# Splitting the queries before their transposes, keeping the keys in two orders, and one way of splitting the transposed probabilities

## The chip, the cores and the metric

The kernel runs on one core of one Trainium2 chip. The metric is device time in microseconds (us) of one execution; three executions of the kernel before are given, with their median. The engines are called as in the profile: PE (TensorE, matrix products and transposes; PEld is its weight load), DVE (VectorE), ACT (ScalarE), POOL (GpSimd) and SP (which issues the DMAs).

## What is computed

The reference is a two-layer transformer in fp32 on 512 tokens of width 1024, with 16 heads of 64. Layer A mixes tokens with three branches of attention over 4 key groups, layer B with sliding-window attention with sinks over 2 key groups; each is followed by a gated feed-forward network with a short convolution. Cut to the part that the change touches, it is:

```python
# layer A, for each block of 128 queries (selection keeps all 8 blocks of 64 keys here)
sc  = einsum('bgrqd,bgnd->bgrqn', qq, kc_h) * dh ** -0.5       # 31 compressed keys
p_c = softmax(where(valid, sc, NEG)) * valid
ss  = einsum('bgrqd,bgqkcd->bgrqkc', qq, k_sel) * dh ** -0.5   # selected keys, causal
sw  = einsum('bgrqd,bgkd->bgrqk', qq, kwb) * dh ** -0.5        # window of 512 keys
out = g0 * (p_c @ vc_h) + g1 * (softmax(ss) @ v_sel) + g2 * (softmax(sw) @ vwb)
# layer B, for each block of 128 queries and the 256 keys around it
sc  = einsum('bnqgrd,bnkgd->bgrnqk', qb, kk) * dh ** -0.5
p   = exp(sc - mx) / (exp(sc - mx).sum() + exp(sink - mx));  o = p @ vv
```

## The kernel before

Every fp32 product is made of float32r products of a rounded part ("hi") and a rounded remainder ("lo"). `weight` (lines 108 to 118) loads a weight tile with a DMA from SP, has ACT round it to `wh` (line 116) and POOL or DVE subtract to `wl` (line 117); `mm3` (lines 101 to 104) then makes three products.

The core runs, in this order: the first projections of layer A (0 to about 100 us); attention A with the other projections woven in (100 to 350 us); feed-forward A (to 745 us); projections of B and attention B (745 to 890 us); feed-forward B.

A head's 64 numbers fill half of the 128 rows that a product sums over, and the kernel uses the other half for the split. The keys are laid as [hi | lo] along the rows: `cat_k` (line 271) makes the two halves (ACT line 198, POOL line 199), `stack_k` (line 277) transposes them (line 282, float32r) and ACT takes them out of PSUM (line 287). The queries are laid twice, as [q | q]: `dup_q` (line 289) copies and scales them on POOL (line 291), `stack_q` (line 295) transposes the copy in fp32 (line 300), ACT rounds the result out of PSUM to `qh` (line 302) and DVE subtracts to `ql` (line 303). The scores are then two products on the same keys, `qh` and then `ql` (lines 710 and 711 in A, 928 and 929 in B, 672 and 673 for the compressed keys).

A unit of attention is a "quad": four heads on a block of 128 queries. Each layer has 16 of them. Its steps in A are `prepare` (`dup_q`), `stack` (`stack_q`), four `head` steps (scores on PE, max on DVE line 722, exponentials on ACT line 733, scaling on POOL line 740), `weigh` (which ends in the split of `pc`, on ACT line 198 and POOL line 199), and a body: `trans(z)` turns probabilities by four fp32 transposes (`probs_t`, line 310) and splits them into `pth` and `ptl`, `product(z)` multiplies them with the values (lines 761 and 762), `ctrans` turns `pc` (line 769), `finish` writes the heads out. In `probs_t` two ways are built in: "V" rounds out of PSUM on ACT (line 314) and subtracts on DVE (line 315); "P" copies out raw on ACT (`ptr`, line 318) and does both steps on POOL (lines 319 and 320). In A the way "P" is taken where `z % 99 == 1`, once in each quad; in B it is never taken.

`weave` merges lists of steps by places between 0 and 1, and the tables `LEAD_A`, `LAG_A`, `PREP`, `CMP` and `FILL_A` place the heads and `weigh` of the next quad, the `stack` of the one after it and the projections among the body of this one. The program text so written gives priorities; a planner then lays out each engine's queue from them, from its own estimate of each instruction's duration and from the time at which a buffer comes free. Each engine runs its queue in order. Tiles with `bufs=2` alternate between two buffers: a writer waits until the readers of the tile two back are done.

Of the kernel before, what the change touches and what calls it, by code (L numbers as in the profile page):

```python
# [17 lines left out]
P = 128  # L18
S = 512
# [18 lines left out]
SPLIT_A = {'out': 'P', 'rope': 'S', 'ropek': 'S', 'kcat': 'P', 'cmp': 'P', 'stack': 'P', 'every': 99}  # L38
SPLIT_B = {'out': 'P', 'rope': 'S', 'kcat': 'P', 'stack': 'P'}
# [33 lines left out]
def hybrid_kernel(ctx, tc, t):  # L73
# [198 lines left out]
    def cat_k(pool, k, n):  # L272

        kc = pool.tile([P, 2, 2, HD], F32R, name="kcat", bufs=2)
        split_sb(kc[:, :n, 0], kc[:, :n, 1], k, "kcat")
        return kc

    def stack_k(dst, kc, n):

        ps = t_tile()  # L280
        for g in range(n):
            pe_tr(ps[:, g * P:(g + 1) * P].bitcast(F32R), kc[:, g].rearrange("p a d -> p (a d)"), identr)
        src = ps[:, :n * P].rearrange("p (g n) -> p g n", g=n)
        if pick["split"]["stack"] == "V":
            nc.vector.tensor_copy(dst, src)
        else:
            nc.scalar.copy(dst, src)

    def dup_q(pool, q):
        qd = pool.tile([P, 4, 2, HD], F32, name="qd", bufs=2)  # L290
        nc.gpsimd.tensor_scalar(qd, q.unsqueeze(2).to_broadcast([P, 4, 2, HD]), SCALE, 1.0,
                                op0=OP.mult, op1=OP.mult)
        return qd

    def stack_q(pool, qd):
        qh = pool.tile([P, 4, P], F32R, name="qh", bufs=2)
        ql = pool.tile([P, 4, P], F32R, name="ql", bufs=2)
        ps = t_tile()
        for r in range(4):
            pe_tr(ps[:, r * P:(r + 1) * P], qd[:, r].rearrange("p a d -> p (a d)"), ident)  # L300
        pv = ps.rearrange("p (r n) -> p r n", r=4)
        nc.scalar.copy(qh, pv)
        nc.vector.tensor_sub(ql, pv, qh.bitcast(F32))
        return qh, ql

    def probs_t(pool, blocks, way="V"):

# [5 lines left out]
        if way == "V":  # L313
            nc.scalar.copy(ph, ps)  # L314
            nc.vector.tensor_sub(pl, ps, ph.bitcast(F32))  # L315
        else:
            raw = pool.tile([P, S], F32, name="ptr", bufs=2)
            nc.scalar.copy(raw, ps)
            nc.gpsimd.tensor_scalar(ph, raw, 1.0, 1.0, op0=OP.mult, op1=OP.mult)
            nc.gpsimd.tensor_sub(pl, raw, ph.bitcast(F32))  # L320
        return ph, pl
# [128 lines left out]
    with tc.tile_pool(name="att_a", bufs=1) as pa, tc.tile_pool(name="att_a2", bufs=1) as pp:  # L450
        gates = pa.tile([P, NT, NH * 3], F32, name="gates")
        KcT = pa.tile([P, P], F32R, name="KcT")
# [18 lines left out]
        def stack_kg(g):  # L471
            def go(i):
                k0 = 32 + i * 2 * P
                stack_k(K[g][:, k0:k0 + 2 * P].rearrange("p (b n) -> p b n", b=2), kcs[g, i], 2)
# [88 lines left out]
        def compress(kv):  # L563
# [50 lines left out]
            def third():  # L614
                if kv == 0:
                    stack_k(KcT.unsqueeze(1), st["kc"], 1)
# [34 lines left out]
        def quad_a(g, i):  # L651
# [5 lines left out]
            def prepare():  # L657
                st["qd"] = dup_q(pp, Q[g][:, i])

            def stack():  # L660
                st["q"] = stack_q(pp, st["qd"])
# [3 lines left out]
            def compressed():  # L665
                qh, ql = st["q"]
                cs = t_tile()[:, 0:P]
                mm(cs, identb, cmask[:, i].unsqueeze(1).to_broadcast([P, 4, 32]), start=True, stop=False)
                for r in range(4):
                    o = cs[:, r * 32:(r + 1) * 32]  # L670
                    kc = KcT[:, g * 32:(g + 1) * 32]
                    mm(o, qh[:, r], kc, start=False, stop=False)
                    mm(o, ql[:, r], kc, start=False, stop=r == 3)
# [11 lines left out]
            def weigh():  # L685
# [5 lines left out]
                st["pc"] = pp.tile([P, 4, 2, 32], F32R, name="pc", bufs=2)  # L691
                split_sb(st["pc"][:, :, 0], st["pc"][:, :, 1], pcb, "cmp")

            def head(r):
                def go():
                    qh, ql = st["q"]
                    sf = s_tile().rearrange("p a n -> p (a n)")
                    if joint and r == 0:
                        if g not in front:
                            front.add(g)  # L700
                            nc.vector.tensor_copy(K[g][:, 0:32], KcT[:, g * 32:(g + 1) * 32])
# [161 lines left out]
    with tc.tile_pool(name="att_b", bufs=1) as pb:  # L863
# [5 lines left out]
        KB = pb.tile([P, GB, NT, P], F32R, name="KB")  # L869
# [30 lines left out]
        weave([lambda i=i: stack_k(KB[:, :, i], kcs[i], GB) for i in range(NT)],  # L900
              [lambda i=i: evac_qb(0)(i, q0_ps(i)) for i in range(NT)], qproj[1][:2])

        with tc.tile_pool(name="att_b2", bufs=1) as pp:
            ot = [xpool.tile([P, NCH // 2, 2, S], F32R, name=n) for n in ("s0", "s2")]

            def quad_b(q, i):
# [5 lines left out]
                def prepare():  # L912
                    st["qd"] = dup_q(pp, Q[q][:, i])

                def stack():
                    st["q"] = stack_q(pp, st["qd"])

                def scores():
                    qh, ql = st["q"]
                    s2 = s_tile()  # L920
                    kk = KB[:, g, k0:k0 + 2].rearrange("p i n -> p (i n)")
                    mk = band if i > 0 else band0
                    for a in range(2):
                        mm(s2[:, a], identb, mk.unsqueeze(1).to_broadcast([P, 2, 256]), start=True, stop=False)
                        for e in range(2):
                            r = 2 * a + e
                            o = s2[:, a, e * 256:(e + 1) * 256]
                            mm(o, qh[:, r], kk, start=False, stop=False)
                            mm(o, ql[:, r], kk, start=False, stop=e == 1)
# [228 lines left out]
```

## Time and profile before

| what | us |
|---|---|
| median of three executions | 1291.32 (1287.09 to 1292.36) |
| the profiled execution | 1289.82 |
| its span, first to last instruction | 1288.0 |
| PE busy in the span | 1246.4 |
| POOL busy | 671.4 |
| DVE busy | 785.8 |
| ACT busy | 631.2 |

The profile names each group of instructions by line, engine, operation and tile (out<-in). "Busy" adds up the durations, and since products follow each other before the one before has ended, a busy PE need not be a PE at its best rate. The chain of waits goes back from the last instruction and gives each moment to the one thing that everything after it waited for.

### The profile page before, as it was taken

To read this page: it belongs to the slowest core of one execution; us is meant where nothing else is said; L and a number is where in the kernel's file an instruction comes from. 1 tells how busy PE (TensorE), PEld (TensorE's weight loads), DVE (VectorE), ACT (ScalarE), POOL (GpSimd) and SP (SyncE) were. 2 spreads that over 40 slices of the span, in tenths; PEclk is the share of its full clock that TensorE was granted. 3 is DMA by queue.
4 is the path that set the end of the run, shared out by engine and by line. 5 is a ranking of instruction groups with operands and counts; after the bars stand their busy time and mean duration, and the time that the engine had idled before them with its cause. 6 is when DMAs were issued, how large, how long until landed. Compare 5 with 4: busy or idle time off the path is not lost.

```text
span 1288.0 us, 17680 instructions
## 1 busy us (share of the span) xinstructions
PE 1246.4 (97%) x6539; PEld 1034.6 (80%) x6539; DVE 785.8 (61%) x1262; ACT 631.2 (49%) x1280; POOL 671.4 (52%) x604
## 2 busy tenths in 40 slices
PE   8999999989999999999999998999999999999997
PEld 7897887768778888888888897987788888888886
DVE  6866766566448774047776456775487831587712
ACT  5657676777445343124434346775453421344432
POOL 4049696867574444444445446765644444444452
PEclk9999999999999999999999999999999999999999
DMA  5441010210032222222222131121222222222221
GB/s 194 135 160 52 2 50 17 73 60 34 33 100 97 93 88 99 98 94 87 98 98 98 49 116 34 34 78 41 95 98 90 91 98 98 91 89 99 98 82 66
DMA packets 34085, 106.45 MB, mean 83 GB/s; under 512 B 4048, under 2 KB 6608, under 8 KB 34000
## 3 DMA queue, kind: packets, MB, share of 16 engines
q1 hardware_dynamic: 34000, 105.34, 24.3%
q8 instruction: 51, 0.84, 0.3%
q14 instruction: 34, 0.28, 0.1%
HBM read 103.23 MB, written 2.10 MB: 82 GB/s over the span
## 4 chain that ended last, share of the span: by engine, by line
PE 84%; DVE 7%; ACT 3%; POOL 3%; issue 2%; DMA 1%; SPq 0%; DVEq 0%; ACTq 0%; POOLq 0%
PE pss L103 14%; PE pss L104 14%; PE pss L102 14%; PE pst L102 10%; PE pst L104 10%; PE pst L103 10%; PE pst L310 3%; DVE s L185 2%; POOL wl L117 1%; PE psv L762 1%; PE pss L710 1%; PE psv L761 1%; PE pss L711 1%; ACT prm L733 1%; PE pst L300 1%
## 5 line engine op out<-in xcount | busy, mean ns | idle before, releaser
L117 POOL TENSOR_TENSOR wl<-wr,wh 128x1024 fp32r<-128x1024 f32 x164 | 395.7, 2413 | 402.5 <-ACT wh L116 402.5
L116 ACT CAST wh<-wr 128x1024 fp32r<-128x1024 f32 (+2 forms) x201 | 197.6, 984 | 347.0 <-issue 170.7
L103 PE MATMUL pss<-s,wh 128*128 128x512 f32 x736 | 292.0, 397 | 3.8 <-DVE s L185 3.8
L102 PE MATMUL pss<-s,wh 128*128 128x512 f32 x736 | 291.3, 396 | 2.3 <-ACT s L198 2.1
L104 PE MATMUL pss<-s,wl 128*128 128x512 f32 x736 | 290.8, 396 | 0.0
L103 PEld LDWEIGHTS pss<-s,wh 128*128 128x128 f32 x736 | 138.3, 188 | 39.4 <-DVE s L185 6.2
L102 PEld LDWEIGHTS pss<-s,wh 128*128 128x128 f32 x736 | 138.1, 188 | 37.1 <-ACT s L198 3.0
L104 PEld LDWEIGHTS pss<-s,wl 128*128 128x128 f32 x736 | 138.3, 188 | 32.8
L104 PE MATMUL pst<-actv,wl 128*128 128x512 f32 (+1 forms) x363 | 141.0, 389 | 0.0
L103 PE MATMUL pst<-actv,wh 128*128 128x512 f32 (+1 forms) x363 | 140.7, 388 | 0.0
L102 PE MATMUL pst<-actv,wh 128*128 128x512 f32 (+1 forms) x363 | 140.2, 386 | 0.0
L415 DVE SCALAR_TENSOR_TENSOR cv<-u,convp,cv 128x512 f32<-128x512 f32 x88 | 123.3, 1439 | 12.9 <-ACT cv L414 12.9
L199 DVE TENSOR_TENSOR actv<-sa,actv 128x512 fp32r<-128x512 f32 x44 | 101.6, 2312 | 30.7 <-ACT actv L198 30.5
L443 DVE TENSOR_TENSOR s<-s,pst 128x512 f32<-128x512 f32 x31 | 21.3, 687 | 152.6 <-PE pst L104 152.6
L412 DVE TENSOR_TENSOR u<-pss,R 128x512 f32<-128x512 f32 x84 | 54.1, 686 | 65.1 <-PE pss L104 65.1
L420 ACT ACTIVATE sa<-cv 128x512 f32<-128x512 f32 x44 | 27.9, 634 | 123.1 <-DVE cv L417 123.0
L103 PEld LDWEIGHTS pst<-actv,wh 128*128 128x128 f32 x363 | 68.4, 188 | 15.1
L102 PEld LDWEIGHTS pst<-actv,wh 128*128 128x128 f32 x363 | 68.4, 188 | 14.8
L104 PEld LDWEIGHTS pst<-actv,wl 128*128 128x128 f32 x363 | 68.4, 188 | 14.0
L315 DVE TENSOR_TENSOR ptl<-pst,pth 128x512 fp32r<-128x512 f32 x92 | 62.3, 686 | 21.5 <-ACT pth L314 20.7
L314 ACT CAST pth<-pst 128x512 fp32r<-128x512 f32 x92 | 53.8, 592 | 37.1 <-PE pst L310 30.6
L414 ACT ACTIVATE cv<-u,convp 128x512 f32<-128x512 f32 x88 | 66.6, 807 | 2.1 <-DVE u L412 2.1
(242 smaller groups left out, 2583.5 us busy)
## 6 DMA issues: line engine op xcount, KB each, us to landing
wr<-fin SPq DMA_DIRECT2D x88, 512.0 KB, 3.2
wr<-fout SPq DMA_DIRECT2D x44, 512.0 KB, 3.2
wr<-wg SPq DMA_DIRECT2D x10, 512.0 KB, 3.2
wr<-cw SPq DMA_DIRECT2D x8, 512.0 KB, 3.3
wr<-woA SPq DMA_DIRECT2D x8, 512.0 KB, 3.2
wr<-woB SPq DMA_DIRECT2D x8, 512.0 KB, 3.2
wr<-wqb SPq DMA_DIRECT2D x6, 512.0 KB, 3.2
s<-xT SPq DMA_DIRECT2D x8, 256.0 KB, 5.6
```

What stands on the lines that cost most here:

```text
L102: mm(out, ah, bh, start=start, stop=False)
L103: mm(out, ah, bl, start=False, stop=False)
L104: mm(out, al, bh, start=False, stop=stop)
L116: nc.scalar.copy(hi[:, :n], raw[:, :n])
L117: engines[next(pick["w"], "P")].tensor_sub(lo[:, :n], raw[:, :n], hi[:, :n].bitcast(F32))
L199: engines[pick["split"][name] if name else "V"].tensor_sub(lo, src, hi.bitcast(F32))
L310: pe_tr(ps[:, r * P:(r + 1) * P], blocks[r], ident)
L314: nc.scalar.copy(ph, ps)
L315: nc.vector.tensor_sub(pl, ps, ph.bitcast(F32))
L412: nc.vector.tensor_mul(u[:, s, 2:], src, norm["R"])
L414: act(cv[:, s], u[:, s, 2:], AF.Identity, bias=par[:, 3:4], scale=par[:, 2:3])
L415: nc.vector.scalar_tensor_tensor(cv[:, s], u[:, s, 1:S + 1], par[:, 1:2], cv[:, s], op0=OP.mult, op1=OP.add)
```

## The change

The queries are split first: `cat_q` rounds q to hi on ACT and subtracts to lo on POOL, both from and to SBUF, on 128x256 numbers, and lays them as [hi | lo]. `stack_q` transposes that in float32r, and one ACT copy takes it out of PSUM as `qt`. The keys are laid out as [hi | lo | hi] by `cat_k` and transposed at two offsets, so that two orders, [hi | lo] and [lo | hi], stand in `K`, `KB` and `KcT`; one DVE instruction takes both out of PSUM and applies the scale. The scores are two products of the same `qt`, with one order and then the other. All probabilities go the way "V". To make room, `kn` in A and `pc` go from two buffers to one.

```diff
-SPLIT_A = {..., 'kcat': 'P', 'cmp': 'P', 'stack': 'P', 'every': 99}
+SPLIT_A = {..., 'kcat': 'P', 'cmp': 'P'}
     def cat_k(pool, k, n):
-        kc = pool.tile([P, 2, 2, HD], F32R, name="kcat", bufs=2)
-        split_sb(kc[:, :n, 0], kc[:, :n, 1], k, "kcat")
+        kc = pool.tile([P, 2, 3, HD], F32R, name="kcat", bufs=2)
+        nc.scalar.copy(kc[:, :n, 0:3:2], k.unsqueeze(2).to_broadcast([P, n, 2, HD]))
+        engines[pick["split"]["kcat"]].tensor_sub(kc[:, :n, 1], k, kc[:, :n, 0].bitcast(F32))
         return kc
     def stack_k(dst, kc, n):
         ps = t_tile()
-        for g in range(n):
-            pe_tr(ps[:, g * P:(g + 1) * P].bitcast(F32R), kc[:, g].rearrange("p a d -> p (a d)"), identr)
-        src = ps[:, :n * P].rearrange("p (g n) -> p g n", g=n)
-        if pick["split"]["stack"] == "V":
-            nc.vector.tensor_copy(dst, src)
-        else:
-            nc.scalar.copy(dst, src)
-    def dup_q(pool, q):
-        qd = pool.tile([P, 4, 2, HD], F32, name="qd", bufs=2)
-        nc.gpsimd.tensor_scalar(qd, q.unsqueeze(2).to_broadcast([P, 4, 2, HD]), SCALE, 1.0,
-                                op0=OP.mult, op1=OP.mult)
-        return qd
+        for o in range(2):
+            for g in range(n):
+                a = (o * n + g) * P
+                pe_tr(ps[:, a:a + P].bitcast(F32R), kc[:, g].rearrange("p a d -> p (a d)")[:, o * HD:o * HD + P], identr)
+        nc.vector.tensor_scalar(dst, ps[:, :2 * n * P].rearrange("p (o g n) -> p o g n", o=2, g=n), SCALE, None, op0=OP.mult)
+    def cat_q(pool, q):
+        qc = pool.tile([P, 4, 2, HD], F32R, name="qc", bufs=2)
+        nc.scalar.copy(qc[:, :, 0], q)
+        nc.gpsimd.tensor_sub(qc[:, :, 1], q, qc[:, :, 0].bitcast(F32))
+        return qc
-    def stack_q(pool, qd):
-        qh = pool.tile([P, 4, P], F32R, name="qh", bufs=2)
-        ql = pool.tile([P, 4, P], F32R, name="ql", bufs=2)
+    def stack_q(pool, qc):
+        qt = pool.tile([P, 4, P], F32R, name="qt", bufs=2)
         ps = t_tile()
         for r in range(4):
-            pe_tr(ps[:, r * P:(r + 1) * P], qd[:, r].rearrange("p a d -> p (a d)"), ident)
-        pv = ps.rearrange("p (r n) -> p r n", r=4)
-        nc.scalar.copy(qh, pv)
-        nc.vector.tensor_sub(ql, pv, qh.bitcast(F32))
-        return qh, ql
+            pe_tr(ps[:, r * P:(r + 1) * P].bitcast(F32R), qc[:, r].rearrange("p a d -> p (a d)"), identr)
+        nc.scalar.copy(qt, ps.rearrange("p (r n) -> p r n", r=4))
+        return qt
-    def probs_t(pool, blocks, way="V"):
+    def probs_t(pool, blocks):
...
-        KcT = pa.tile([P, P], F32R, name="KcT")
+        KcT = pa.tile([P, 2, P], F32R, name="KcT")
-            K.append(pa.tile([P, 32 + NT * 2 * P], F32R, name="Kg", bufs=2))
+            K.append(pa.tile([P, 2, 32 + NT * 2 * P], F32R, name="Kg", bufs=2))
-                kn = pa.tile([P, 2, HD], F32, name="kn", bufs=2)
+                kn = pa.tile([P, 2, HD], F32, name="kn", bufs=1)
-                st["pc"] = pp.tile([P, 4, 2, 32], F32R, name="pc", bufs=2)
+                st["pc"] = pp.tile([P, 4, 2, 32], F32R, name="pc", bufs=1)
-                        mm(o, qh[:, r], K[g][:, k0 + a:k0 + b], start=True, stop=False)
-                        mm(o, ql[:, r], K[g][:, k0 + a:k0 + b], start=False, stop=b < n0 and not joint)
+                        mm(o, qt[:, r], K[g][:, 0, k0 + a:k0 + b], start=True, stop=False)
+                        mm(o, qt[:, r], K[g][:, 1, k0 + a:k0 + b], start=False, stop=b < n0 and not joint)
-                    pt[z] = probs_t(pp, [st["pr"][r][:, k, b] for r in range(4)],
-                                    "P" if z % SPLIT_A["every"] == 1 else "V")
+                    pt[z] = probs_t(pp, [st["pr"][r][:, k, b] for r in range(4)])
-        KB = pb.tile([P, GB, NT, P], F32R, name="KB")
+        KB = pb.tile([P, 2, GB, NT, P], F32R, name="KB")
```

The compressed scores (lines 672 and 673) and those of B (928 and 929) change as those of A do, the copy of `KcT` to the front of `Kg` (line 701) takes both orders, and `prepare` calls `cat_q` in place of `dup_q`.

## Rows read from the trace of the kernel before

**Rows 1.** The page's first part: busy time of each engine over the span, with its share and the number of instructions.

```profile
PE 1246.4 (97%) x6539; PEld 1034.6 (80%) x6539; DVE 785.8 (61%) x1262; ACT 631.2 (49%) x1280; POOL 671.4 (52%) x604
```

**Rows 2.** Busy time by stretch (us from the span's start, length, then for PE, PEld, DVE, ACT and POOL busy us and instructions, the granted PE clock, DMA share, GB/s): attention A, feed-forward A, attention B in two parts, and then four quarters of attention A.

```profile
100.00:350.00 250.00, 236.75 (x1535) 195.27 (x1534) 154.93 (x384) 172.56 (x514) 186.59 (x277) 0.99 0.12 41
350.00:745.00 395.00, 392.55 (x1735) 318.13 (x1734) 241.18 (x252) 156.28 (x206) 183.52 (x83) 1.00 0.27 91
760.00:780.00 20.00, 17.24 (x135) 15.86 (x133) 13.22 (x39) 9.47 (x31) 13.38 (x14) 1.00 0.23 80
780.00:890.00 110.00, 105.67 (x679) 91.91 (x680) 73.17 (x176) 73.28 (x207) 70.70 (x108) 1.00 0.14 44
...
100.00:125.00 25.00, 22.20 (x145) 17.58 (x144) 16.37 (x51) 20.11 (x68) 23.16 (x39) 0.93 0.19 64
125.00:150.00 25.00, 23.25 (x166) 20.00 (x164) 20.14 (x46) 20.80 (x66) 22.66 (x38) 1.00 0.00 1
175.00:200.00 25.00, 23.84 (x162) 19.17 (x160) 18.09 (x48) 23.11 (x71) 24.19 (x35) 1.00 0.13 43
225.00:250.00 25.00, 22.77 (x175) 19.80 (x174) 14.41 (x45) 17.91 (x56) 23.05 (x34) 1.00 0.13 44
```

**Rows 3.** The chain of waits by line, first in attention A (100 to 350 us), then in attention B (755 to 890 us): share of the stretch.

```profile
by line: PE pst L310 9.7%; PE pst L102 9.5%; PE pst L104 9.0%; PE pst L103 9.0%; PE psv L762 5.7%; PE psv L761 5.7%; PE pss L710 5.7%; PE pss L711 5.0%; ACT prm L733 4.4%; issue 3.8%; POOL wl L117 2.6%; DVE nmx L722 2.4%; POOL prl L740 2.3%
...
by line: PE pst L102 13.4%; PE pst L103 12.7%; PE pst L104 12.6%; POOL wl L117 6.9%; PE pst L310 6.5%; PE pss L929 4.8%; PE pss L928 4.6%; PE psv L963 4.2%; PE psv L962 4.1%; PE pst L300 3.9%; PE pss L924 3.7%; DVE stat L938 3.1%; issue 2.2
```

**Rows 4.** Transposes: first by line, with count and duration in ns (min/median/max); then two neighbouring pieces of the chain of waits at the start of B (start us, us, what), in which each transpose counts from the start of one to the start of the next.

```profile
L300 PEld LDWEIGHTS pst<-cst,qd x128: 137/140/143, 88.1 to 865.2; 128*128 128x128 f32 x128
L300 PE MATMUL pst<-cst,qd x128: 270/272/329, 88.1 to 865.3; 128*128 128x128 f32 x128
L282 PEld LDWEIGHTS pst<-identr,kcat x41: 138/141/237, 74.3 to 766.1; 128*128 128x128 f32 x41
L282 PE MATMUL pst<-identr,kcat x41: 221/228/454, 74.4 to 766.1; 128*128 128x128 f32 x41
...
766.24 0.13 PE pst L282 x2
766.37 0.46 PE pst L300 x4
```

**Rows 5.** Groups by form over the whole span: shapes, count, busy us, mean ns of one, then the idle time before them and what ended it.

```profile
L302 ACT CAST qh<-pst 128x512 fp32r<-128x512 f32 x32 | 19.0, 594 | 9.4 <-PE pst L300 8.8
L303 DVE TENSOR_TENSOR ql<-pst,qh 128x512 fp32r<-128x512 f32 x32 | 21.9, 685 | 5.1 <-ACT qh L302 4.6
L291 POOL TENSOR_SCALAR qd<-Qb 128x512 f32<-128x512 f32 x16 | 10.0, 623 | 9.7 <-PE pst L300 7.6 <-DVE Qb L215 2.0 <-PE pst L310 0.2
L198 ACT CAST s<-osum 128x256 fp32r<-128x256 f32 x32 | 13.2, 412 | 8.6 <-DVE osum L331 8.3
L199 POOL TENSOR_TENSOR s<-osum,s 128x256 fp32r<-128x256 f32 x32 | 23.7, 740 | 19.5 <-ACT s L198 19.5
L319 POOL TENSOR_SCALAR pth<-ptr 128x512 fp32r<-128x512 f32 x16 | 9.9, 620 | 4.3 <-ACT ptr L318 4.0 <-DVE ptl L315 0.2
L320 POOL TENSOR_TENSOR ptl<-ptr,pth 128x512 fp32r<-128x512 f32 x16 | 20.6, 1286 | 0.4
L315 DVE TENSOR_TENSOR ptl<-pst,pth 128x512 fp32r<-128x512 f32 x92 | 62.3, 686 | 21.5 <-ACT pth L314 20.7
L287 ACT CAST Kg<-pst 128x256 fp32r<-128x256 f32 x16 | 6.1, 382 | 0.6 <-PE pst L282 0.6
L198 ACT CAST kcat<-kn 128x128 fp32r<-128x128 f32 x20 | 6.1, 306 | 0.9 <-DVE kn L215 0.5 <-POOL kn L215 0.4
```

**Rows 6.** Pieces of the chain of waits (start us, us, what) in both layers: first the split of the queries on DVE, the first and the last of five pieces (0.60, 0.61, 0.70, 0.70 and 0.61 us); then the copy of the queries on POOL (both pieces); then the two POOL steps of the way "P" (both); then the copy of the keys out of PSUM on ACT (the first and the last of three, 0.27, 0.27 and 0.37 us).

```profile
106.24 0.60 DVE ql L303
803.80 0.61 DVE ql L303
...
98.05 0.59 POOL qd L291
197.06 0.59 POOL qd L291
...
199.15 0.59 POOL pth L319
201.40 1.24 POOL ptl L320
...
181.91 0.27 ACT Kg L287
255.91 0.37 ACT Kg L287
```

**Rows 7.** Instructions in order of time (start us, us, engine, line). The key tile `kn` of the fourth token block and the split of the third and fourth key tiles, at the start of A; then the first and the last of four pairs in which ACT writes the next quad's `pc` before PE has turned this quad's.

```profile
83.15 0.28 DVE L215 TENSOR_TENSOR kn<-rope,rope 128x128 f32<-128x128 f32 x1
87.23 0.91 POOL L199 TENSOR_TENSOR kcat<-kn,kcat 128x128 fp32r<-128x128 f32 x2
...
208.37 0.30 ACT L198 CAST pc<-pcb 128x128 fp32r<-128x128 f32 x1
210.93 0.28 PE L769 MATMUL pst<-identr,pc 128*128 128x128 f32 x2
...
309.97 0.33 ACT L198 CAST pc<-pcb 128x128 fp32r<-128x128 f32 x1
312.27 0.29 PE L769 MATMUL pst<-identr,pc 128*128 128x128 f32 x2
```

More of the change, by code (lines that the diff above doesn't have):

```diff
@@ L37 @@
 W_B = 8 * "V"
-SPLIT_A = {'out': 'P', 'rope': 'S', 'ropek': 'S', 'kcat': 'P', 'cmp': 'P', 'stack': 'P', 'every': 99}
-SPLIT_B = {'out': 'P', 'rope': 'S', 'kcat': 'P', 'stack': 'P'}
+SPLIT_A = {'out': 'P', 'rope': 'S', 'ropek': 'S', 'kcat': 'P', 'cmp': 'P'}
+SPLIT_B = {'out': 'P', 'rope': 'S', 'kcat': 'P'}
 LEAD_A = [0.21, 0.02, 0.72, 0.53, 0.59, 0.42, 0.4, 0.11, 0.02, 0.99, 0.65, 0.43, 0.05, 0.42, 1.02, 0.48]
@@ L312, in probs_t @@
         pl = pool.tile([P, S], F32R, name="ptl", bufs=2)
[L313 to L320, printed above, removed]
+        nc.scalar.copy(ph, ps)
+        nc.vector.tensor_sub(pl, ps, ph.bitcast(F32))
         return ph, pl
@@ L615, in third @@
                 if kv == 0:
-                    stack_k(KcT.unsqueeze(1), st["kc"], 1)
+                    stack_k(KcT.unsqueeze(2), st["kc"], 1)
                     return
@@ L657, in prepare @@
             def prepare():
-                st["qd"] = dup_q(pp, Q[g][:, i])
+                st["qc"] = cat_q(pp, Q[g][:, i])
             def stack():
-                st["q"] = stack_q(pp, st["qd"])
+                st["q"] = stack_q(pp, st["qc"])
                 st["sums"] = small.tile([P, 4, 2], F32, name="sums")
@@ L665, in compressed @@
             def compressed():
-                qh, ql = st["q"]
+                qt = st["q"]
                 cs = t_tile()[:, 0:P]
@@ L670, in compressed @@
                     o = cs[:, r * 32:(r + 1) * 32]
-                    kc = KcT[:, g * 32:(g + 1) * 32]
-                    mm(o, qh[:, r], kc, start=False, stop=False)
-                    mm(o, ql[:, r], kc, start=False, stop=r == 3)
+                    kc = KcT[:, :, g * 32:(g + 1) * 32]
+                    mm(o, qt[:, r], kc[:, 0], start=False, stop=False)
+                    mm(o, qt[:, r], kc[:, 1], start=False, stop=r == 3)
                 csv = cs.rearrange("p (r b) -> p r b", r=4)
@@ L695, in go @@
                 def go():
-                    qh, ql = st["q"]
+                    qt = st["q"]
                     sf = s_tile().rearrange("p a n -> p (a n)")
@@ L700, in go @@
                             front.add(g)
-                            nc.vector.tensor_copy(K[g][:, 0:32], KcT[:, g * 32:(g + 1) * 32])
+                            nc.vector.tensor_copy(K[g][:, :, 0:32], KcT[:, :, g * 32:(g + 1) * 32])
                         st["pcb"] = pp.tile([P, 4, 32], F32, name="pcb", bufs=2)
@@ L899, in hybrid_kernel @@
         warm_exp(r_nat[:, 0:1])
-        weave([lambda i=i: stack_k(KB[:, :, i], kcs[i], GB) for i in range(NT)],
+        weave([lambda i=i: stack_k(KB[:, :, :, i], kcs[i], GB) for i in range(NT)],
               [lambda i=i: evac_qb(0)(i, q0_ps(i)) for i in range(NT)], qproj[1][:2])
@@ L912, in prepare @@
                 def prepare():
-                    st["qd"] = dup_q(pp, Q[q][:, i])
+                    st["qc"] = cat_q(pp, Q[q][:, i])
                 def stack():
-                    st["q"] = stack_q(pp, st["qd"])
+                    st["q"] = stack_q(pp, st["qc"])
                 def scores():
-                    qh, ql = st["q"]
+                    qt = st["q"]
                     s2 = s_tile()
-                    kk = KB[:, g, k0:k0 + 2].rearrange("p i n -> p (i n)")
+                    kk = [KB[:, o, g, k0:k0 + 2].rearrange("p i n -> p (i n)") for o in range(2)]
                     mk = band if i > 0 else band0
@@ L927, in scores @@
                             o = s2[:, a, e * 256:(e + 1) * 256]
-                            mm(o, qh[:, r], kk, start=False, stop=False)
-                            mm(o, ql[:, r], kk, start=False, stop=e == 1)
+                            mm(o, qt[:, r], kk[0], start=False, stop=False)
+                            mm(o, qt[:, r], kk[1], start=False, stop=e == 1)
                     st["sv"] = s2.rearrange("p a (e n) -> p (a e) n", e=2)
```

2 lines of the change are left out of this document (1 added, 1 removed).

## The prediction

> **What bounds the kernel now.** I read the shares of the engines first. PE is busy for 97% of the span [rows 1], so a change must either take work from PE or shorten the few waits that PE has. The next view is busy time by stretch. In feed-forward A PE is idle for 2.5 of 395 us, and nothing of the change lies there. In attention A (100 to 350 us) PE is idle for 13.3 of 250 us, in attention B (760 to 890 us) for 2.8 + 4.3 = 7.1 of 130 us [rows 2]. These two stretches hold all that moves. In four quarters of A POOL is busy for 22.7 to 24.2 of 25 us, and in the same four PE is idle for 2.8 + 1.8 + 1.2 + 2.2 = 8.0 us; in the first of them the granted clock is 0.93, elsewhere in these rows 0.99 or 1.00 [rows 2]. The third view is the chain of waits: in A most of it is PE's own work, and of the shares in the row that are not PE's, ACT has 4.4%, DVE 2.4% and POOL 4.9%; in B POOL's weight splitting has 6.9% and DVE's max 3.1% [rows 3]. So PE's work counts nearly in full, POOL's and DVE's only where they stand on the chain.
>
> **PE's own work.** The scores keep their number, shape and kind of products, so they cost what they did; that both now use one weight tile saves nothing, since `mm3` already uses one tile twice in a row and the trace has as many loads as products [rows 1]. What changes is the transposes. The 128 of the queries go from fp32 to float32r: four fp32 ones take 0.46 us of the chain and two float32r ones 0.13 us [rows 4], so a group of four falls from 0.46 to 0.26, and 32 groups save 6.4 us. The keys get a second set: 16 tiles of A and 4 of B with two more each, and the compressed keys with one more, 41 in all [rows 4], at 0.065 us 2.7 us more. Net 3.7 us less; the piece of 0.46 is a long one, and with the 0.44 that four steps of 0.11 give it is 5.8 - 2.7 = 3.1. PE is busy for 95% of both stretches, so I take **2.9 us less**.
>
> Here a rule speaks against the change. The rows show two float32r transposes in 0.13 us although each has a weight load of 141 ns, as long as the 140 ns of the fp32 kind [rows 4], so the load does not set the pace there. The Trainium skill, page "TensorE: Matmul & The Clock Gate", section "Back-to-back issue gap", says that in a real kernel the spacing of products is set by the load and the product together, and gives about 81 ns at 128 columns. By that figure, an estimate, the queries would save 32 x (0.44 - 0.32) = 3.8 us and the keys cost 3.3, so that almost nothing would be left. The row is of this very instruction and I go by it; the mechanism is a rival below.
>
> **The queries.** On DVE 32 subtractions of 685 ns go, on ACT 32 copies of 256 columns at 412 ns come, on POOL 32 copies of 623 ns become 32 subtractions at 740 ns [rows 5]; the ACT copy out of PSUM stays at 594 ns for `qt` as for `qh`. Scores then wait for one copy in place of a copy and a subtraction. The subtraction stands on the chain five times, 3.2 us together [rows 6], and nothing takes its place: **3.2 us less**, with 0 as the other end if another engine is ready no earlier. The POOL copy is on the chain twice with 0.59 us [rows 6]. There the new steps are 0.41 + 0.74 = 1.15 us, so **1.1 us more**. At the other 30 quads `prepare` runs two quads ahead and that covers it; without that cover it would be 30 x 0.53 = 16 us, but the same cover holds for the present copy. ACT's copy and POOL's subtraction stand in front of the exponentials and of the scaling of the probabilities in their queues.
>
> **The probabilities.** In each of A's 16 quads POOL loses 0.62 + 1.29 us, 30.6 us in all, and DVE gets a subtraction of 686 ns, 11.0 us [rows 5], as much as it loses with the queries; ACT's copy stays. With the queries' 16 x 0.12 us more, POOL falls by 28.7 of its 186.6 us in A [rows 2, 5]. Directly on the chain stand only 0.59 and 1.24 us of it [rows 6], against one subtraction of 0.69 in their place, 1.1 us less. The rest is the queue: in the four full quarters the weight splits and the scaling of the probabilities wait behind these steps. What PE loses there is 8.0 us [rows 2], and the ends are 1.1 us and all 8.0. POOL has 4.9 of the 11.7% that the three engines have in the row of the chain [rows 3], so I take that share of 8.0: **3.3 us less**, the 1.1 included.
>
> **The keys.** ACT loses 20 copies of 382 ns, DVE gets 20 copies out of PSUM of twice the size; the nearest row is the subtraction of that size out of PSUM, 686 ns [rows 5], so 13.7 us more on DVE, 11.0 of them in A. ACT's first copy is 128x256 in place of 128x128, 412 against 306 ns [rows 5]. The evacuation is on the chain three times with 0.9 us [rows 6]; at 0.69 each that is 2.1, so **1.3 us more** with one slower first copy. The other 17 are hidden behind heads whose keys were stacked before; if they were not, they would cost up to 11.7 us, which I keep for the range. Summed up, DVE in A goes from 155 to 166 of 250 us and ACT from 173 to 175; in B DVE falls by 8 and ACT rises by 5.5 of 130 us. Neither becomes full. The front copy of `KcT` doubles in size four times; I count nothing for it.
>
> **The buffers.** With one `kn`, its next writer waits until ACT and POOL have read the last. At the start of A DVE writes the `kn` of the fourth block at 83.15 us, and POOL splits the third's only at 87.23 to about 87.7 [rows 7]: up to 4.5 us in which DVE stands, and behind it in its queue the values' split and the weight splits that `W_A` gives to DVE at that time; PE waits for those weights. The planner knows the buffer and can put other work first, so I take **1.0 us more**. With one `pc`, ACT's copy for the next quad waits until PE has turned this quad's. Now it comes earlier in four of fifteen pairs, by 2.2 to 2.8 us from its start to the end of the transposes, 10.1 us together [rows 7]; behind it in ACT's queue stand the exponentials that free the score banks. The next `pc` is needed only a quad later, so the planner can move it at no cost: 0, with 10.1 as the other end.
>
> **The sum** is -2.9 - 3.2 + 1.1 - 3.3 + 1.3 + 1.0 = -6.0 us. The profiled execution took 1289.8 us, 1.8 more than its span, and would take 1283.8; the median of the runs is 1.5 us above it, so the forecast is 1285 us, about half a per cent below 1291.3.
>
> **The rivals.** (1) POOL was the cause of all that PE loses in the four full quarters, and the evacuations and buffers cost nothing: -3.1 - 3.2 + 1.1 - 8.0 = -13.2, 1278 us. For it speak the POOL shares above 90%; against it that ACT's exponentials have as much of the chain as POOL. (2) The waits stay: where the query split and POOL go, the next engine is as late, as the softmax goes from PE to DVE to ACT and back: -2.9 + 1.1 + 1.3 + 1.0 = +0.5, 1292 us. For it speaks that the pieces on the chain are short and change from engine to engine. (3) The weight load sets the pace of the float32r transposes too: no saving on 128, and 41 at 0.11 us: +4.5 in place of -2.9, 1293 us; the pair in 0.13 us speaks against it [rows 4], and it is the rule of the page named above. (4) Slower: one buffer where there were two makes DVE stand at the start of A and ACT stand in each quad, 4.5 + 10.1 = 14.6 in place of 1.0: +7.6, 1299 us. It decides only if some 13.5 of the 14.6 us come through to PE, and the planner would have to leave the present order.
>
> **How the numbers follow.** A measurement of this kernel can tell about 0.5%, 6.5 us, from no change, that is, below 1284.9 or above 1297.8. The forecast has 0.45 with 1281 to 1290 of its own, 0.20 of it below 1284.9; rival 1 has 0.25, rival 2 0.13, rival 3 0.05, rival 4 0.12. So faster 0.20 + 0.25 = 0.45, same 0.25 + 0.13 + 0.05 = 0.43, slower 0.12. The range leaves out rival 4 and the low tail of rival 1 and goes from 1275 to 1297 us.
>
> **What would show it.** Four query transposes should take about 0.26 us of the chain and PE's busy time should fall by some 3 us; `ql` should be gone from the chain; POOL should be busy for about 158 us in A and under 90% in the four quarters, with PE's idle time there near 4.7 us; the evacuation of the keys should last about 690 ns on DVE. I am wrong if PE's idle time in A stays at 13 us or more though POOL has emptied, if ACT is seen waiting for PE's transposes of `pc`, or if DVE waits for POOL's key split near 83 us.

## The result and the profile after

The changed kernel takes 1300.5 us (median of five runs, 1296.9 to 1303.2) beside 1290.7 us for the kernel before in the same job: a ratio of 1.0067, with a 95% interval from 1.0047 to 1.0087. That is 8.7 us more by the ratio, with the wrong sign and above the end of the range at 1297. The profiled execution took 1301.6 us, 1.8 more than its span of 1299.8.

The page's first part, which answers to [rows 1]:

```profile
PE 1253.7 (96%) x6580; PEld 1041.7 (80%) x6580; DVE 790.4 (61%) x1267; ACT 635.2 (49%) x1291; POOL 645.2 (50%) x572
```

PE has 41 instructions more, as the diff says, but 7.3 us more busy time, and it is idle for 46.1 us of the span where it was idle for 41.6. POOL has lost 26 us, close to the prediction, and the span has grown all the same. So the reader looks for the stretch in which PE lost time.

Busy time by stretch of the changed kernel, columns as in [rows 2]. The first row is the start of attention A, which [rows 2] does not show; the rest answers to it:

```profile
75.00:100.00 25.00, 20.36 (x158) 19.79 (x157) 12.64 (x28) 11.69 (x22) 10.96 (x10) 0.89 0.44 148
100.00:350.00 250.00, 239.74 (x1585) 200.71 (x1584) 164.54 (x415) 173.50 (x525) 160.59 (x251) 0.98 0.11 39
...
350.00:745.00 395.00, 392.47 (x1701) 316.02 (x1700) 237.82 (x252) 154.56 (x204) 185.11 (x84) 1.00 0.27 90
760.00:780.00 20.00, 18.71 (x159) 18.18 (x158) 14.53 (x41) 6.87 (x13) 12.37 (x12) 1.00 0.31 106
780.00:890.00 110.00, 103.37 (x695) 90.20 (x694) 68.09 (x172) 80.13 (x236) 74.66 (x110) 1.00 0.13 44
...
100.00:125.00 25.00, 22.99 (x174) 19.97 (x172) 17.62 (x61) 14.72 (x49) 18.16 (x29) 0.98 0.14 44
125.00:150.00 25.00, 22.74 (x123) 17.51 (x124) 17.28 (x39) 20.79 (x65) 18.27 (x31) 0.86 0.06 22
175.00:200.00 25.00, 24.33 (x183) 20.84 (x183) 17.81 (x46) 17.61 (x57) 18.18 (x31) 1.00 0.14 44
225.00:250.00 25.00, 25.00 (x192) 22.49 (x191) 14.54 (x40) 15.47 (x46) 15.95 (x23) 1.00 0.13 43
```

The same row of the kernel before, and of two kernels told of below (the changed one with two buffers of `kn`, and that with one key order as well), one fence each:

```profile
75.00:100.00 25.00, 24.47 (x210) 23.89 (x209) 16.16 (x49) 15.16 (x39) 14.98 (x18) 1.00 0.43 145
```

```profile
75.00:100.00 25.00, 22.84 (x197) 22.23 (x196) 16.61 (x44) 12.81 (x25) 12.30 (x14) 1.00 0.44 152
```

```profile
75.00:100.00 25.00, 24.44 (x210) 23.92 (x210) 14.63 (x52) 14.60 (x35) 15.39 (x19) 1.00 0.46 149
```

Between 75 and 100 us PE was idle for 0.5 us and is now idle for 4.6, and it issues 158 products where it issued 210. The granted clock falls to 0.89 in this quarter and to 0.86 in the one from 125 us; before it stood at 1.00 in both (in the quarter between them it was 0.93 [rows 2] and is 0.98). In feed-forward A, 350 to 745 us, PE is as busy as before. POOL is busy for 160.6 us in A, near the 158 predicted, and what was forecast to follow from that is there: in the four quarters of [rows 2] PE is idle for 4.9 us (4.7 forecast, 8.0 before), and in all of A for 10.3 where it was 13.3, though a PE at a lower clock is also busy for longer. The loss begins ahead of them, from 75 us, which the prediction left out when it wrote of A from 100 us and of B: "These two stretches hold all that moves."

What PE waits for at the start of A is in the chain of waits of the changed kernel (start us, us, what):

```profile
85.81 1.49 POOL wl L117
87.31 0.74 issue
88.05 2.36 POOL wl L117
90.41 0.42 POOL kcat L276
90.83 0.04 issue
90.88 0.55 PE pst L285 x4
```

and in its instructions in order of time (start us, us, engine, line, what, idle time before and its releaser), which answer to [rows 7]:

```profile
83.60 0.28 DVE L215 TENSOR_TENSOR kn<-rope,rope 128x128 f32<-128x128 f32 x1
...
88.67 0.39 ACT L275 CAST kcat<-kn 128x256 fp32r<-128x256 f32 x1
90.37 0.45 POOL L276 TENSOR_TENSOR kcat<-kn,kcat 128x128 fp32r<-128x128 f32 x1
90.86 0.29 DVE L215 TENSOR_TENSOR kn<-rope,rope 128x128 f32<-128x128 f32 x1
90.88 0.53 PE L285 MATMUL pst<-identr,kcat 128*128 128x128 f32 x4 [1.65 <-POOL kcat L276]
...
92.38 0.40 ACT L275 CAST kcat<-kn 128x256 fp32r<-128x256 f32 x1
...
93.31 0.39 PE L702 MATMUL pss<-Kg,qt 128*128 128x256 f32 x1 [1.57 <-ACT qt L301]
...
94.86 0.45 POOL L276 TENSOR_TENSOR kcat<-kn,kcat 128x128 fp32r<-128x128 f32 x1
95.36 0.75 PE L285 MATMUL pst<-identr,kcat 128*128 128x128 f32 x4 [1.42 <-POOL kcat L276]
```

ACT has its copy of the third key tile at 89.06, but POOL's remainder of the same tile starts at 90.37, behind its weight splits, and PE waits 1.65 us. `kn` has one buffer, so DVE writes the fourth key tile at 90.86, when POOL has let go of the third. Before, DVE wrote the fourth tile at 83.15, 4 us ahead of POOL's remainder of the third [rows 7]. With the fourth tile not ready, PE waits 1.57 us for `qt`; the fourth remainder stands behind another weight split and ends at 95.3, and PE waits 1.42 us for it. A key tile now has to pass through POOL's queue before the next may be written. This can happen with the first key group only: its four tiles are written by DVE, the other twelve of A by POOL itself, in the same queue as the remainder.

The three waits don't have one cause. With two buffers of `kn` (an experiment below) the same instructions read

```profile
91.46 0.53 PE L288 MATMUL pst<-identr,kcat 128*128 128x128 f32 x4 [1.65 <-POOL kcat L279]
...
92.18 0.50 PE L288 MATMUL pst<-identr,kcat 128*128 128x128 f32 x4
```

so the first wait is still there, as long as before, and only the other two, 3.0 us together, are the single buffer's.

### The profile page after: what moved, and what is told of

Same layout as the page of the kernel before. It is cut to its first block, busy times and chain, and to the rows that moved or that the text cites. A ratio compares the mean times of both kernels' runs of the same rounds, so it can differ in the third digit from the quotient of the medians.

```text
span 1299.8 us, 17807 instructions
## 1 busy us (share of the span) xinstructions
PE 1253.7 (96%) x6580; PEld 1041.7 (80%) x6580; DVE 790.4 (61%) x1267; ACT 635.2 (49%) x1291; POOL 645.2 (50%) x572
## 4 chain that ended last, share of the span: by engine, by line
PE 84%; DVE 7%; ACT 4%; POOL 2%; issue 2%; DMA 1%; SPq 0%; DVEq 0%; ACTq 0%; POOLq 0%
PE pss L103 14%; PE pss L104 14%; PE pss L102 14%; PE pst L102 10%; PE pst L103 10%; PE pst L104 10%; PE pst L308 3%; DVE s L185 2%; PE psv L753 1%; PE psv L752 1%; POOL wl L117 1%; PE pss L702 1%; PE pss L703 1%; DVE s L339 1%; ACT prm L725 1%
## 5 line engine op out<-in xcount | busy, mean ns | idle before, releaser
L312 DVE TENSOR_TENSOR ptl<-pst,pth 128x512 fp32r<-128x512 f32 x108 | 73.5, 687 | 28.9 <-ACT pth L311 28.1
L311 ACT CAST pth<-pst 128x512 fp32r<-128x512 f32 x108 | 63.5, 597 | 40.6 <-PE pst L308 32.0
```

## The experiments

All were timed in five rounds beside the kernel before, and the microseconds below are a ratio less one, times 1291. The theories that the expectations name: **Theory 1**, the one buffer of `kn`, read by POOL. **Theory 2**, the second order of the keys: 2a by PE's transposes, 2b by the larger evacuation and the longer way to the first query. **Theory 3**, neither: the planner's order comes out otherwise with any change, and moves the time by some 4 us.

**One buffer of `kn`, alone,** in the kernel before:

```diff
-                kn = pa.tile([P, 2, HD], F32, name="kn", bufs=2)
+                kn = pa.tile([P, 2, HD], F32, name="kn", bufs=1)
```

> The kernel before with one change alone: the key tile kn of attention A has one buffer in place of two. Theory 1 (the single kn buffer makes DVE, and behind it the key splits, late at the start of A, PE then idles and its clock falls): slower than before by 5 to 9 us, with PE idle time between 75 and 100 us up by some 4 us. Theory 2 (the doubled key transposes, the larger evacuation on DVE and the longer way of the first queries make the start of A late): within 2 us of before. Theory 3 (any edit makes the planner lay another order, worth several us either way): a shift of up to 4 us of either sign, not at the start of A in particular.

Measured: 1296.2 us, ratio 1.0043 (1.0029 to 1.0057), 5.6 us more. One number in the old kernel gives more than half of the loss.

**One buffer of `pc`, alone,** in the kernel before (the same edit on `st["pc"]`):

> The kernel before with one change alone: pc has one buffer in place of two. Theory 1, for pc (ACT waits for the transposes of pc in four of fifteen quads): slower by 2 to 5 us. Theory 2: within 2 us of before, since pc is needed a quad later and the planner moves it. Theory 3: up to 4 us of either sign.

Measured: 1291.6 us, ratio 1.0004 (0.9995 to 1.0012). It costs nothing that can be measured.

**All probabilities by ACT and DVE, alone,** in the kernel before:

```diff
-                                    "P" if z % SPLIT_A["every"] == 1 else "V")
+                                    "V")
```

> The kernel before with one change alone: all transposed probabilities are split by ACT and DVE. The prediction's step on POOL: faster by 1 to 8 us, 3.3 taken, POOL busy 30 us less in A. Its rival (the waits stay, since DVE gets the work that POOL loses and the softmax goes through DVE): within 2 us of before, or slower by up to 4 us.

Measured: 1289.6 us, ratio 0.9992 (0.9982 to 1.0003). POOL falls from 186.6 to 158.6 us in A, and that alone is worth 1 us, 2 at most, in the time (what the clock has to do with it is told with the last experiments).

**Two buffers of `kn` in the changed kernel** (the room comes from the tile of ones, which is cut to three columns):

```diff
-                kn = pa.tile([P, 2, HD], F32, name="kn", bufs=1)
+                kn = pa.tile([P, 2, HD], F32, name="kn", bufs=2)
```

> The changed kernel with two kn buffers again; the room comes from the tile of ones, of which 2 of 128 columns are kept (the first warm-up products read a constant laid in the space of convp). Theory 1: faster than the changed kernel by 6 to 9 us, so about 1291 to 1294 us, and PE idles no longer for 1.6 us twice at 91 and 95 us. Theory 2: still 1298 to 1301 us. Theory 3: 1294 to 1302 us.

Measured: 1292.5 us, ratio 1.0009 (0.9998 to 1.0020), 7.5 us under the changed kernel. The row of the quarter from 75 us, shown above, gives PE 2.5 us back, and the clock stays at 1.00 there; the quarter from 125 us has 0.86 here too. Of the two waits for `kcat` the one at 95 us is gone and the one at 91 us is not, where the expectation had both gone.

**The remainder of the keys on DVE in A, `kn` still with one buffer:**

```diff
-SPLIT_A = {'out': 'P', 'rope': 'S', 'ropek': 'S', 'kcat': 'P', 'cmp': 'P'}
+SPLIT_A = {'out': 'P', 'rope': 'S', 'ropek': 'S', 'kcat': 'V', 'cmp': 'P'}
```

> The changed kernel, still with one kn buffer, but in attention A the remainder of the keys (the subtraction in cat_k) is made by DVE in place of POOL. Theory 1 in its sharper form (the single kn buffer costs because its reader on POOL stands behind 2.4 us weight splits): 1292 to 1295 us, some 6 us faster than the changed kernel. Rival (one buffer costs as such, whichever engine reads it, or DVE's added load costs as much): 1298 to 1301 us.

Measured: 1291.3 us, ratio 1.0006 (0.9997 to 1.0015), 7.9 us under the changed kernel. The single buffer costs nothing as soon as its reader doesn't stand behind POOL's weight splits. **Both remedies together:**

> The changed kernel with two kn buffers and the remainder of A's keys on DVE. If waits of the key split behind POOL's weight splits are what is left at the start of A (PE still idles 1.6 us there for kcat): 2 to 3 us faster than a_kn2, 1289 to 1290 us. Rival (DVE is full at the start of A and the load comes back): within 1 us of a_kn2.

Measured: 1291.3 us, ratio 1.0004 (0.9993 to 1.0014). The second adds nothing to the first, which fits two remedies of one wait. The wait that is left is not shortened by much: PE stands 1.38 us for DVE's remainder in place of 1.65 for POOL's.

**The queries' transposes in fp32 again** (with two buffers of `kn`):

```diff
-            pe_tr(ps[:, r * P:(r + 1) * P].bitcast(F32R), qc[:, r].rearrange("p a d -> p (a d)"), identr)
+            pe_tr(ps[:, r * P:(r + 1) * P], qc[:, r].rearrange("p a d -> p (a d)").bitcast(F32), ident)
```

> The changed kernel with two kn buffers, its queries transposed in fp32 in place of float32r. The prediction's step (a float32r transpose counts 0.065 us against 0.11): slower than a_kn2 by 5 to 6 us, PE busy up by as much. Rival (float32r transposes in a row of four count 0.08 us, as the timeline of the changed kernel reads): slower by 3 to 4 us. If transposes hide behind waits: no difference.

Measured: 1290.9 us, ratio 1.0005 (0.9996 to 1.0014), beside 1.0009 with float32r. The float32r transposes save nothing that shows in the time, where the prediction had 5.8 to 6.4 us.

**One key order in the changed kernel** (with two buffers of `kn`; half the key transposes, evacuation of 128x256):

```diff
-        for o in range(2):
+        for o in range(1):
...
-        nc.vector.tensor_scalar(dst, ps[:, :2 * n * P].rearrange("p (o g n) -> p o g n", o=2, g=n), SCALE, None, op0=OP.mult)
+        nc.vector.tensor_scalar(dst[:, 0], ps[:, :n * P].rearrange("p (g n) -> p g n", g=n), SCALE, None, op0=OP.mult)
```

> The changed kernel with two kn buffers and without the second order of the keys: 41 transposes and half of each evacuation are left out, and the scores multiply the first order twice, so that the cross terms of hi and lo are left out of the result. If the second order costs what its PE work is: 41 x 0.08 = 3.3 us faster than a_kn2. The prediction's step: 2.7 us of PE and up to 1 us of evacuation. If it is hidden: within 1.5 us of a_kn2.

Measured: 1283.7 us, ratio 0.9954 (0.9939 to 0.9968). Against 1.0009 the second order costs 7.1 us, and without it the change would gain 5.9. PE is idle for 0.6 us between 75 and 100 us, as before the change.

**The doubled transposes alone,** in the kernel before:

```diff
-        for g in range(n):
-            pe_tr(ps[:, g * P:(g + 1) * P].bitcast(F32R), kc[:, g].rearrange("p a d -> p (a d)"), identr)
+        for o in range(2):
+            for g in range(n):
+                a = (o * n + g) * P
+                pe_tr(ps[:, a:a + P].bitcast(F32R), kc[:, g].rearrange("p a d -> p (a d)"), identr)
```

> The kernel before, and each key group's transposes are made twice, into the second half of the same PSUM bank; only the first half is evacuated, as before. So it adds 82 instructions on PE (41 groups go from two transposes to four, two of them with fewer) and nothing on any other engine. Theory 2a (the pace of the transposes): a group of four took 0.34 us and a pair 0.127 us in the changed kernel, so this costs 41 x 0.21 us less what lies in idle time of PE, between 1291 + 3.7 and 1291 + 8.6, about 1296. Theory 2b (what the second order costs is the larger evacuation and the longer way to the first query, not PE): 1291 to 1293.

Measured: 1297.9 us, ratio 1.0056 (1.0042 to 1.0071), 7.2 us more. The expectation counts 41 groups; there are 41 more transposes, in some 20 groups, so the pace alone explains only 20 x 0.17 = 3.4 us of it (0.17 from the rows below). Some of the rest lies where the changed kernel's first wait does: from 75 to 100 us PE is busy for 22.9 us instead of 24.5, and it stands for the same POOL remainder, in this kernel's instructions in order of time:

```profile
91.42 0.53 PE L284 MATMUL pst<-identr,kcat 128*128 128x128 f32 x4 [1.66 <-POOL kcat L199]
93.16 0.38 PE L102 MATMUL pst<-wh,s 128*128 128x256 f32 x1 [0.45 <-ACT Kg L289]
```

The evacuation here is the old one, so the doubled transposes alone give the price of the second order; how much of it beyond the 3.4 us is the order that the planner then laid is not separated.

**The evacuation of the keys on DVE, alone,** in the kernel before (`'stack': 'V'` in `SPLIT_A`):

> The kernel before, and the keys' transposes are evacuated by DVE where ACT did it, in the old size (128x256). It prices the move of the evacuation alone. Theory 2a expects nothing of it (within 1 us of the kernel before): both engines have idle time in stage A. Theory 2b expects some of the loss here: 32 instructions of 0.42 us on an engine that also makes the maxima and the remainders, 1292 to 1294.

Measured: 1293.7 us, ratio 1.0017 (1.0005 to 1.0029), 2.2 us more, for 16 evacuations of keys in A, not the 32 of the expectation. **The doubled evacuation on ACT,** in the changed kernel with the key remainder on DVE:

> The changed kernel with the key remainder of stage A on DVE (1291.3), and the doubled evacuation (128x512, scaled) on ACT in place of DVE. Theory 2a: no difference, 1290 to 1292. Theory 2b: DVE's 32 evacuations of 0.69 us are in the way of the maxima and remainders, so 1288 to 1290; the other way about if ACT's exponentials are what the heads wait for, 1293.

Measured: 1291.4 us, ratio 1.0002 (0.9990 to 1.0013), beside 1.0006 with DVE. Moving the evacuation to DVE costs 2.2 us in the one kernel and 0.5 in the other, about as far apart as the intervals allow; the engine of the evacuation is a matter of 2 us or less.

**Both loads off POOL, without the new orders,** in the kernel before (all probabilities by ACT and DVE, and `'kcat': 'V'`):

> The kernel before, with all transposed probabilities split by ACT and DVE and the key remainder of stage A on DVE: both loads that the change and the experiments took off POOL, without the new order of keys and queries. If POOL's queue is what keys and queries wait for in the kernel before too, it is 1286 to 1289; if two buffers of kn hide that wait already, it is where all probabilities on ACT and DVE alone were, 1289 to 1291.

Measured: 1291.4 us, ratio 0.9996 (0.9983 to 1.0008). With two buffers of `kn` the wait for POOL was hidden already.

That left the gain of 5.9 us without a cause. **No remainder of the queries,** in the kernel before:

```diff
-        nc.vector.tensor_sub(ql, pv, qh.bitcast(F32))
-        return qh, ql
+        return qh, qh
```

> The kernel before without the queries' remainder: DVE makes no ql, and the second score product of each head reads qh once more, so its result leaves out the low part of the queries. PE's instructions are all there. It prices what the change takes off DVE and off the way to the scores by splitting ahead of the transposes. By the sum of the prediction, 1291 - 3.2 = 1288. By the balance of the runs so far (the changed kernel with two kn and one key order is 7 us under the kernel before, of which the probabilities are 1) it must be 5 to 6, so 1285. If ql is hidden, 1291, and the 7 us lie elsewhere.

Measured: 1294.1 us, ratio 1.0025 (1.0015 to 1.0036): 3.2 us more for less work, which only theory 3 leaves room for. **And with all probabilities by ACT and DVE:**

> The same, with all transposed probabilities split by ACT and DVE as well. With ql away, DVE has the room for them: by the balance 1284, as the changed kernel with two kn and one key order (1283.7); if the gain of that kernel came from its float32r transposes or its queries' copies instead, 1287 to 1291.

Measured: 1284.3 us, ratio 0.9947 (0.9932 to 0.9961), 6.8 us less. The two parts of the gain don't add: -1.0 and +3.2 alone, -6.8 together. Busy time by stretch (columns as in [rows 2]) without `ql`, probabilities partly on POOL:

```profile
100.00:125.00 25.00, 21.08 (x141) 16.06 (x139) 17.61 (x50) 20.13 (x68) 23.75 (x40) 1.00 0.20 65
125.00:150.00 25.00, 24.66 (x163) 21.34 (x164) 15.09 (x41) 20.43 (x65) 21.27 (x35) 0.93 0.00 1
...
175.00:200.00 25.00, 21.21 (x137) 17.16 (x135) 14.22 (x34) 21.06 (x61) 23.12 (x34) 0.95 0.14 43
200.00:225.00 25.00, 25.00 (x172) 22.49 (x173) 15.10 (x40) 15.01 (x51) 14.65 (x28) 0.91 0.00 1
```

and without `ql`, all probabilities on ACT and DVE:

```profile
100.00:125.00 25.00, 23.09 (x160) 18.07 (x158) 18.89 (x53) 21.20 (x72) 22.86 (x39) 1.00 0.19 65
125.00:150.00 25.00, 24.50 (x170) 20.63 (x168) 17.77 (x48) 19.95 (x64) 15.76 (x29) 1.00 0.00 1
...
175.00:200.00 25.00, 21.32 (x142) 17.02 (x141) 17.04 (x40) 20.48 (x59) 20.27 (x29) 1.00 0.13 43
200.00:225.00 25.00, 24.52 (x178) 21.47 (x179) 16.59 (x43) 16.24 (x55) 11.82 (x23) 1.00 0.01 2
```

In the first, DVE has 46.9 us of work in the three of these quarters that [rows 2] shows, where it had 54.6, and POOL is nearly as full as before (68.1 and 70.0). PE stands for 3.9 and 3.8 us in two quarters, and the clock is below 1.00 in three, which takes 25 x (0.07 + 0.05 + 0.09) = 5.2 us of full speed where the kernel before lost 25 x 0.07 = 1.8. In the second POOL is emptier as well, and the clock is 1.00 in all four.

These are two profiled executions, but each execution has its granted clock on record, and they say the same. Full speed missing, (1 - clock) x span, is 7.6 us in the kernel before (mean of 101 executions), 11.4 without `ql` (10), 10.2 with all probabilities on ACT and DVE (11), and 6.2 with both edits (6). In the kernel before alone, the 40 executions at 0.993 have a median of 1292.35 us and the 15 at 0.996 one of 1289.38: 3.0 us for 3.9 us of full speed. Counted one for one, an estimate from these numbers, an equal clock leaves -0.6 without `ql`, -3.6 with the probabilities moved and -5.4 with both. So most of what doesn't add is the clock: the probabilities' gain was there alone too, and the clock took most of it back. Why the clock is lower in the two single edits was not tried.

## Why the prediction was wrong

Three steps of differences lead from the kernel before to the changed one: everything but the second order and the single buffer, -5.9 us; the second order, +7.1; the single `kn`, +7.5; together +8.7. The parts tried in the kernel before give about the same: -6.8 (`ql` and probabilities together), +7.2 and +5.6, in sum +6.0. The prediction's terms, sorted in the same way, miss all three on the same side:

| step | terms of the prediction | measured |
|---|---|---|
| all but the second order and the single `kn` | -5.5 (query transposes) - 3.2 + 1.1 - 3.3 = -10.9 | -5.9 |
| the second order of the keys | +2.6 (transposes) + 1.3 (evacuation) = +3.9 | +7.1 |
| the single `kn` | +1.0 | +7.5 |
| sum | -6.0 | +8.7 |

**The single `kn` is the step that failed first.** The prediction saw the wait, its place and its length ("up to 4.5 us in which DVE stands"), and priced it at 1.0 because "the planner knows the buffer and can put other work first". It measured 5.6 us alone and 7.5 in the changed kernel. The planner did put scores first, and PE waited for them as well. The 4.5 us were no upper bound either. With the single buffer PE is idle for 46.1 us of the span, with two for 41.7; and the mean of full speed missing is 11.2 us with one and 9.2 with two, so of the 7.5 us some 4.4 are waits and 2.0 the clock. Rival 4 named this mechanism and gave 1299 us, but in large part for another reason: it wanted most of the 10.1 us of `pc`, of which none came. That its number is near the measured one is luck.

**PE's own work is the second.** The prediction had -2.9 us. Instructions of PE in order of time in the kernel before, each group of transposes with the instruction that follows it:

```profile
188.20 0.28 PE L282 MATMUL pst<-identr,kcat 128*128 128x128 f32 x2
188.32 0.47 PE L710 MATMUL pss<-Kg,qh 128*128 128x512 f32 x1
...
181.04 0.37 PE L282 MATMUL pst<-identr,kcat 128*128 128x128 f32 x2
181.24 0.46 PE L761 MATMUL psv<-pth,Vg 128*128 128x512 f32 x1
...
129.08 0.60 PE L300 MATMUL pst<-cst,qd 128*128 128x128 f32 x4
129.44 0.48 PE L762 MATMUL psv<-ptl,Vg 128*128 128x512 f32 x1
```

and in the changed kernel:

```profile
122.67 0.45 PE L285 MATMUL pst<-identr,kcat 128*128 128x128 f32 x4
122.96 0.46 PE L702 MATMUL pss<-Kg,qt 128*128 128x512 f32 x1
...
126.20 0.54 PE L285 MATMUL pst<-identr,kcat 128*128 128x128 f32 x4
126.58 0.63 PE L308 MATMUL pst<-cst,prl 128*128 128x128 f32 x4
...
215.48 0.45 PE L300 MATMUL pst<-identr,qc 128*128 128x128 f32 x4
215.77 0.46 PE L752 MATMUL psv<-pth,Vg 128*128 128x512 f32 x1
...
158.45 0.54 PE L300 MATMUL pst<-identr,qc 128*128 128x128 f32 x4
158.82 0.46 PE L752 MATMUL psv<-pth,Vg 128*128 128x512 f32 x1
```

What counts is the time from the start of a group to the start of the next instruction. Two float32r transposes take 0.12 or 0.20 us, four take 0.29 or 0.37: the third and fourth cost 0.17 us, not 0.13, so the keys cost some 20 x 0.17 = 3.4 us. Four fp32 ones mostly take 0.36, not the 0.44 to 0.46 that the prediction took from a piece of the chain; such a piece ends where a waiting engine is released, not where PE goes on. Over all groups of the queries that ran at full clock with no wait behind them, 26 before and 22 after, the means are 0.39 us in fp32 and 0.33 in float32r, so 32 groups save 1.8 us and not 5.8. The net is about +1.6 in place of -2.9. In the time even that does not show: the kernel with fp32 transposes has less full speed missing (6.3 us, mean of its executions, beside 9.2). Here the Trainium skill, page "TensorE: Matmul & The Clock Gate", section "Back-to-back issue gap", with its 81 ns at 128 columns was nearer than the row of a pair: 0.17 us for two more. Rival 3, which rested on it, was named and given 0.05.

Beyond that PE stands 1.65 us for the third key tile when the transposes are doubled, in the changed kernel with one `kn` or two and in the kernel before (1.66), and not with one key order, where PE is idle for 0.6 us in the whole quarter. The prediction had no term for this. With the clock, of which 9.2 us are missing with the second order and 6.6 without (means), 3.4 + 1.65 + 2.6 = 7.6 us is near the 7.1, an estimate; why the third tile comes late, and what lowers the clock, was not tried.

**The queries and the probabilities** were sized at -3.2 and -3.3; together they give -6.8. Alone they give +3.2 and -1.0, and at an equal clock, by the estimate above, -0.6 and -3.6. So the probabilities were sized about right, the queries were worth little by themselves, and no term stood for the clock; that the sum fits is partly luck. The copies of the queries, +1.1, would fit the difference between -6.8 and -5.9, which is inside both intervals.

**The keys' evacuation** takes 686 ns, as predicted, in the group by form of the changed kernel that answers to [rows 5]:

```profile
L286 DVE TENSOR_SCALAR Kg<-pst 128x512 fp32r<-128x512 f32 x16 | 11.0, 686 | 3.7 <-PE pst L285 3.7
```

and its price of +1.3 lies inside the interval of the move alone (+0.6 to +3.7 us), which doesn't show that it was right: in the changed kernel DVE in place of ACT costs 0.5. **The single `pc`** at 0 was right.

Theory 3 isn't ruled out as a part: kernels that differ by little, such as the one without `ql`, move by 3 us, most of it by the clock. But 7.5 to 7.9 us come back with either of two edits aimed at the `kn` wait, and 5.6 are lost by the single buffer alone; an accident of order would hardly agree three times.

## What to carry to other kernels

Before a buffer is halved, look up the engine that reads it last and what is queued ahead of that reader; a read of half a microsecond that stands behind 2.4 us instructions holds the buffer for as long as they last, and moving the reader to the writer's own engine was worth as much here as the second buffer. Price a run of PE instructions from the start of its first to the start of whatever follows, in a group of the length that the change makes. Read the granted clock of every execution beside its time: here it hid a gain of some 3 us, and made two edits look as if they were worth something only together.

## What the runs showed of the hardware

**POOL can hold DVE.** In the kernel before with one `kn`, instructions in order of time:

```profile
84.66 2.40 POOL L117 TENSOR_TENSOR wl<-wr,wh 128x1024 fp32r<-128x1024 f32 x1 [3.12 <-ACT wh L116]
...
87.02 0.48 POOL L199 TENSOR_TENSOR kcat<-kn,kcat 128x128 fp32r<-128x128 f32 x1
87.47 2.35 POOL L117 TENSOR_TENSOR wl<-wr,wh 128x1024 fp32r<-128x1024 f32 x1
87.54 2.42 DVE L215 TENSOR_TENSOR kn<-rope,rope 128x128 f32<-128x128 f32 x1 [0.35 <-POOL kcat L199]
```

DVE's write of `kn`, 0.28 us at other places [rows 7], starts 0.07 us after POOL's weight split and ends 0.14 us after it: 2.42 us. So in that kernel the freed buffer is refilled only after the next split. The same shows in the two feed-forward parts of the kernel before: of 44 subtractions on DVE with both inputs in SBUF (`actv`, line 199) four take 0.69 us, and the 40 that start during a weight split of POOL take 2.47. The Trainium skill, page "SBUF — State Buffer", section "Who interferes with whom", says that DVE and GpSimd share a pair of ports, which one holds alone; these rows agree.

**The clock is a second price.** Over the whole span of the profiled executions the granted clock was 0.991 in the changed kernel and 0.996 before, so (1 - 0.991) x 1299.8 = 11.7 us of full speed were missing and 5.2 before. That pair overstates it, since this execution of the kernel before has one of its higher clocks: by the means of all executions it is 11.2 and 7.6, so some 3.6 of the 8.7 us. In the changed kernel the row from 125 us has 0.86, so about 0.28 of that quarter was at 1.2 GHz in place of 2.4, and the two quarters ahead of it have PE idle for 4.6 and 2.0 us. Idle time in a quarter doesn't decide alone: with two `kn` the clock is 0.86 there as well, after 2.2 and 2.6 us, and without `ql` and with all probabilities on ACT and DVE, PE stands for 3.7 us from 175 us and the clock stays at 1.00. What in those waits brings it down is left open.
